# Two SwiGLU feed-forward blocks on one core: a first down part of two groups, and a first Strassen group without down parts

## The chip, the core and the metric

The kernel runs on one core of one Trainium2 chip. The metric is the device time of one execution in microseconds (us), as a median over runs. The engines are named as in the profile: PE (TensorE, matmuls; PEld its weight loads), DVE (VectorE), ACT (ScalarE), POOL (GpSimd) and SP (SyncE, which here only issues DMAs).

## The reference, cut to what matters

One decoder layer on 512 tokens with a model width of 1024. The layer has a feed-forward block (FFN1), a token mixer, a second feed-forward block (FFN2), a gated embedding and a last norm. The change touches only the two feed-forward blocks:

```
def rmsnorm(x, g):
    y = x * rsqrt(mean(x * x) + EPS)
    return y * g

def swiglu(x, w_gate, w_up, w_down):
    return (silu(x @ w_gate) * (x @ w_up)) @ w_down

h = h + 0.5 * swiglu(rmsnorm(h, ffn_norm), w_gate, w_up, w_down)     # D_FF = 2816
```

## The kernel before

**Layout.** Features lie on the 128 partitions and the 512 tokens along the free axis, so h is 8 tiles of 128x512. Float32 products are made of three passes: a weight tile is split into whi (ACT casts it to fp32r, line 416) and wlo (DVE subtracts, line 420), and PE adds whi*xhi, whi*xlo and wlo*xhi. The third of these matmuls is the first that needs wlo. There are three whi and three wlo buffers, and one of each in a second pair, whix and wlox, which most down parts use.

**Groups.** The 2816 hidden features of a feed-forward block are 11 groups of 256. Group 0 is computed plainly, in four products of 24 matmuls with 512 columns (`plain_steps`): gate and up, each with the upper and the lower half of the features. The other groups are computed with a Strassen scheme: seven products P1 to P7 (`Group.steps`), each of 24 matmuls with 256 columns (line 603). Their inputs are sums and differences of halves of x ("forms") and of weight blocks. In FFN1 the forms are made step by step (`Early`, lines 514 to 545), in FFN2 beforehand except one (`t1`, lines 462 to 466). The weight sums are partly made by POOL DMAs that add in place (lines 618, 621 and, after P6's split, 655), and one by DVE (line 613).

**Behind a group's products** come the elementwise steps of `Group`: `seed` (ACT, line 717), `keep_p7` and `keep_u2` (ACT, 721 and 725), for each half a gate sum (DVE, 735), the gate's product with r (DVE, 740), silu (ACT, 741), a product with r (DVE, 745), `finish` with the up part (DVE, 750), and at the end `parts_of_g`, which splits the group's g into ghi (ACT, 760) and glo (DVE, 761). r is the norm's factor per token: `Norm.behind` hangs its three steps on three successive products: sums over the features (PE, line 261), then rsqrt and a diagonal matrix (DVE, 217 to 222 and 280) spread by PE (291), then a copy of r (ACT, 297) with group 0's gate (`plain_gate`, DVE 707, ACT 708). Group 0's g is completed by `plain_finish` (DVE, 713 and 714) and split by `parts_of_g`. A g tile has one buffer, tag "g".

**Down parts.** The down projection is done in six parts over the hidden features. `G_PARTS = (1, 2, 2, 2, 2, 2)` says how many groups each holds. A part is four down steps, each for two of the 8 output tiles: 12 matmuls of 512 columns for each group in the part. A down step loads its weights into rawd (two buffers), splits them, and afterwards DVE adds the result to h (line 795). It is queued some steps after its groups are done: part 0 (group 0 alone) lies among the products of groups 1 and 2, part 1 (groups 1 and 2) among those of groups 3 and 4, and so on. Within a group the order is 1, 7, down, 6, 4, 5, down, 2, 3; for group 1 it is 1, 7, 2, 6, 4, down, 5, down, 3.

**The order of work** is written out by hand. `run` walks through the list of steps. While product i is put into PE's queue, the weights of step i+6 are put into SP's queue, the split of step i+2 and the DVE sum of step i+3 into those of ACT and DVE, and the "after" work of step i-1 likewise: ahead of the split if step i-1 is marked urgent (P1, P7, P6, P3 and the lower plain products), behind it otherwise. A second after-function, where there is one, comes two products later, ahead of both. PE, ACT, DVE and SP each execute in that order; POOL's DMAs are placed by the scheduler.

**Banks.** PSUM has three "mm" banks for the x and q sums of the groups (and one plain up product), two single banks a0 and a1, and three "sm" banks for down steps and norms. A new mm tile takes the bank that was given back first: in this program the q tiles of the groups 1 to 10 lie in one bank throughout and the x tiles in the two others by turns.

## Time and profile before

| | us |
|---|---|
| median of 3 runs | 1108.12 |
| lowest, highest | 1106.18, 1108.39 |
| the profiled execution, its own time | 1107.29 |
| its span, first to last instruction | 1105.6 |
| DVE busy | 783.3 |
| ACT busy | 520.6 |

The profiled execution spends 1.7 us outside its span. The profile's lines give the line number in the kernel, the engine, the operation and the tiles ("out<-in"), so "DVE L420 wlo<-rawb,whi" is the split of a weight tile that lay in rawb. In a timeline, the first column is the start in us from the span's start, the second the length, and the bracket at the end tells how long the engine was idle before the instruction and what released it. Instructions on one engine may overlap slightly, so that the distance from start to start is what an instruction costs its queue. FFN1's plain products begin at 18 us, its Strassen groups at 45; FFN2's Strassen groups begin at 733.

### The profile page before, as it was taken

The numbers are of one execution on the slowest core, as the hardware profiler recorded it, in microseconds if no ns is written. First come the engines' busy times: TensorE is split into PE (matmuls) and PEld (weight loads), VectorE is DVE, ScalarE is ACT, GpSimd is POOL, SyncE is SP. The second block draws the span as 40 slices with busy tenths as digits, with TensorE's granted clock in tenths as the row PEclk, the third lists the DMA queues.
The fourth block names the chain that finished last, engine by engine and source line by source line (L and its number), as shares of the span: only waits on it lengthen the run. The fifth ranks groups of instructions, "written<-read, shape, count | busy, mean of one in ns | idle before, by whom it ended". The sixth has DMA issues, their size and how long they took to land.

```text
span 1105.6 us, 16432 instructions
## 1 busy us (share of the span) xinstructions
PE 1083.8 (98%) x6639; PEld 956.4 (87%) x6639; DVE 783.3 (71%) x1066; ACT 520.6 (47%) x715; POOL 136.9 (12%) x130
## 2 busy tenths in 40 slices
PE   9989999999999999999979999999999999999997
PEld 7879999999998788787858888889999999999887
DVE  6887776766666686766878665768767766667766
ACT  5645444444444455474564343454443443434554
POOL 2001000000000300143213100000000000000311
PEclk9999999999999999999989999999999999999999
DMA  9667757566623322444422323477667667543412
GB/s 365 191 170 205 194 152 191 159 190 155 168 58 114 95 95 80 133 134 134 134 76 77 95 77 114 141 183 202 184 186 191 181 177 185 154 133 108 140 51 77
DMA packets 49036, 161.66 MB, mean 146 GB/s; under 512 B 5568, under 2 KB 5824, under 8 KB 48960
## 3 DMA queue, kind: packets, MB, share of 16 engines
q1 hardware_dynamic: 34128, 117.46, 31.0%
q0 software_dynamic: 9232, 33.56, 16.9%
q10 hardware_dynamic: 5600, 9.60, 2.9%
q8 instruction: 52, 0.85, 0.3%
q14 instruction: 24, 0.20, 0.1%
HBM read 156.33 MB, written 4.26 MB: 145 GB/s over the span
## 4 chain that ended last, share of the span: by engine, by line
PE 85%; DVE 8%; ACT 4%; issue 2%; DMA 0%; SPq 0%; DVEq 0%; ACTq 0%
PE mm L603 18%; PE a L603 14%; PE sm L200 10%; PE sm L201 10%; PE sm L199 10%; PE mm L200 4%; PE mm L199 4%; PE mm L201 4%; PE a L199 3%; PE a L201 3%; PE a L200 3%; DVE wlo L420 1%; ACT whi L416 1%; PE sm L261 1%; DVE tmp L1591 1%
## 5 line engine op out<-in xcount | busy, mean ns | idle before, releaser
L416 ACT CAST whi<-raw 128x1024 fp32r<-128x1024 f32 x138 | 144.3, 1046 | 171.1 <-issue 60.2
L420 DVE TENSOR_TENSOR wlo<-raw,whi 128x1024 fp32r<-128x1024 f32 x137 | 172.9, 1262 | 67.8 <-ACT whi L416 63.9
L603 PE MATMUL mm<-xfb,whi 128*128 128x256 f32 x960 | 166.3, 276 | 0.0
L603 PEld LDWEIGHTS mm<-xfb,whi 128*128 128x128 f32 x960 | 145.9, 188 | 1.6
L603 PE MATMUL mm<-xfb,wlo 128*128 128x256 f32 x480 | 132.8, 277 | 0.0
L201 PE MATMUL sm<-ghi,wlox 128*128 128x512 f32 x296 | 116.3, 393 | 0.0
L200 PE MATMUL sm<-glo,whix 128*128 128x512 f32 x296 | 115.9, 391 | 0.0
L199 PE MATMUL sm<-ghi,whix 128*128 128x512 f32 x296 | 115.1, 389 | 0.0
L603 PE MATMUL a<-xfb,whi 128*128 128x256 f32 x640 | 111.1, 276 | 0.0
L603 PEld LDWEIGHTS a<-xfb,whi 128*128 128x128 f32 x640 | 97.7, 188 | 1.9 <-issue 0.2
L603 PEld LDWEIGHTS mm<-xfb,wlo 128*128 128x128 f32 x480 | 90.1, 188 | 0.0
L603 PE MATMUL a<-xfb,wlo 128*128 128x256 f32 x320 | 88.6, 277 | 0.3 <-DVE wlo L420 0.3
L420 DVE TENSOR_TENSOR wlox<-rawd,whix 128x1024 fp32r<-128x1024 f32 (+1 forms) x40 | 45.7, 1141 | 57.6 <-ACT whix L416 57.6
L420 DVE TENSOR_TENSOR wlo<-rawb,whi 128x1024 fp32r<-128x1024 f32 x52 | 63.6, 1223 | 20.8 <-ACT whi L416 20.8
L741 ACT ACTIVATE g<-g 128x512 f32<-128x512 f32 x40 | 25.3, 632 | 110.8 <-DVE g L740 110.8
L795 DVE SCALAR_TENSOR_TENSOR h<-sm,h 128x512 f32<-128x512 f32 x96 | 63.3, 684 | 6.4 <-PE sm L201 5.7
L416 ACT CAST whi<-rawb 128x1024 fp32r<-128x1024 f32 x52 | 54.2, 1043 | 26.4 <-DVE rawb L613 19.7
L618 POOL DMA_DIRECT2D raw<-in_ffn_gu x20 | 17.4, 869 | 395.5 <-DMA raw<-in_ffn_gu 100.0
L201 PEld LDWEIGHTS sm<-ghi,wlox 128*128 128x128 f32 x296 | 55.5, 188 | 11.7
L200 PEld LDWEIGHTS sm<-glo,whix 128*128 128x128 f32 x296 | 55.5, 188 | 10.9
L199 PEld LDWEIGHTS sm<-ghi,whix 128*128 128x128 f32 x296 | 55.6, 188 | 10.7
L603 PEld LDWEIGHTS a<-xfb,wlo 128*128 128x128 f32 x320 | 60.1, 188 | 0.7 <-DVE wlo L420 0.5
(413 smaller groups left out, 2527.9 us busy)
## 6 DMA issues: line engine op xcount, KB each, us to landing
raw<-in_ffn_gu SPq DMA_DIRECT2D x56, 512.0 KB, 6.0
rawd<-in_ffn_down SPq DMA_DIRECT2D x40, 512.0 KB, 4.0
rawb<-in_ffn_gu SPq DMA_DIRECT2D x32, 512.0 KB, 5.3
raw<-in_ffn_gu POOLq DMA_DIRECT2D x30, 512.0 KB, 5.5
raw<-in_w_in SPq DMA_DIRECT2D x29, 512.0 KB, 3.6
s<-in_ffn_gu SPq DMA_DIRECT2D x20, 512.0 KB, 7.2
s<-in_ffn_gu POOLq DMA_DIRECT2D x20, 512.0 KB, 8.5
raw<-in_w_out SPq DMA_DIRECT2D x16, 512.0 KB, 3.6
```

The costliest lines, as they stand in the source:

```text
L199: nc.tensor.matmul(ps, whi, xhi, start=first, stop=False)
L200: nc.tensor.matmul(ps, whi, xlo, start=False, stop=False)
L201: nc.tensor.matmul(ps, wlo, xhi, start=False, stop=last)
L261: nc.tensor.matmul(ps[:, c : c + 1], part[:, c * P : (c + 1) * P], ones[:, 0:1], start=part is t, stop=part is not t or more is None,)
L416: nc.scalar.copy(self.hi[:, : self.n], self.raw[:, : self.n])
L420: nc.vector.tensor_tensor(self.lo[:, :n], self.raw[:, :n], self.hi[:, :n].bitcast(F32), ALU.subtract)
L603: nc.tensor.matmul(o, wt[:, c], xt, start=fresh and p == m == n == 0, stop=last and n == 2, skip_group_check=True,)
L618: nc.gpsimd.dma_start(w21.raw, self.src[0], accum_op=ALU.add)
L741: nc.scalar.activation(t, t, AF.Silu)
L795: nc.vector.scalar_tensor_tensor(h[d], ps[d], 0.5, h[d], ALU.mult, ALU.add)
L1591: engine.tensor_tensor(t, t, emb[d][:, tok], ALU.mult)
```

## The change

The first two parts change places: part 0 now holds groups 0 and 1, part 1 group 2 alone. The order of the steps is written out as strings: group 1 runs 1, 7, 2, 6, 4, 5 without a down step; then comes P1 of group 2, then P3 of group 1; then group 2's 7, 6, down, 4, 5, down, 2, 3, down; then group 3's 1, down, 7, down, 6, 4, 5, down, 2, 3; from group 4 on the order is as before. The numbers of matmuls, splits and additions to h are the same.

In FFN1 (`at` is now 2 instead of 1) the three steps of the norm are hung one product later: the sums come after the last plain product instead of before it. Group 0's g lies in the tile "embt" instead of "g" (embt held embedding results that POOL stores to DRAM early). `plain_finish` is queued with the split of P5 instead of P4, and group 0's `parts_of_g` behind P3 of group 1, after that group's own `finish` and split, instead of behind P2. In FFN2 (`at` is 0 before and after) these stay where they were. The host's layout of the down weights follows G_PARTS.

```
-G_PARTS = (1, 2, 2, 2, 2, 2)
+G_PARTS = (2, 1, 2, 2, 2, 2)
...
         def plain_gate(self):
-            self.g = sb("g", (P, 2, 2, HT))
+            self.g = sb(self.shared["g0"], (P, 2, 2, HT))
...
-        shared = {}
+
+        shared = {"g0": "embt" if at else "g"}
...
         steps = groups[0].plain_steps()
-        g0, pending = 0, []
+
+
+        g0, downs = 0, []
         for part, n in enumerate(G_PARTS):
-            if part:
-                for j in range(g0, g0 + n):
-
-                    here = pending[: -(-len(pending) // (g0 + n - j))]
-                    pending = pending[len(here) :]
-                    for i in (1, 7, 2, 6, 4, 5, 3) if j == 1 else (1, 7, 6, 4, 5, 2, 3):
-                        steps.append(gs[j][i])
-                        if i in ((5, 4) if j == 1 else (7, 5)):
-                            steps.append(here.pop(0))
             g0 += n
             last = part == len(G_PARTS) - 1
-            each = 2
             mine = groups[g0 - n : g0]
-            pending = [down(part, mine, i, each, last) for i in range(ND // each)]
-        steps += pending
+            downs += [down(part, mine, i, 2, last) for i in range(ND // 2)]
+        order = [(1, "172645"), (2, "1"), (1, "3"), (2, "76d45d23d"), (3, "1d7d645d23")]
+        order += [(j, "17d645d23") for j in range(4, len(groups))]
+        for j, products in order:
+            for i in products:
+                steps.append(downs.pop(0) if i == "d" else gs[j][int(i)])
+        steps += downs
...
         if at:
-            also(steps[8], "split", groups[0].plain_finish)
+            also(steps[9], "split", groups[0].plain_finish)
         else:
             also(steps[3], "after", groups[0].plain_finish)
-        also(steps[6 if at else 4], "after", lambda: groups[0].parts_of_g(slice(0, 2)))
+        also(steps[11 if at else 4], "after", lambda: groups[0].parts_of_g(slice(0, 2)))
...
     steps, mix_norm = swiglu(
         "ffn1", x_ffn1, ffn1_norm, lambda: open_region("left", "mix_left"),
-        splitter("mix_norm", x_mix), 1,
+        splitter("mix_norm", x_mix), 2,
     )
```

## The prediction

> **What bounds the kernel now.** I read the page first, then the waits of PE between 30 and 70 us, then busy time by stretch, then the timelines of DVE and ACT there.

> ```profile
> span 1105.6 us, 16432 instructions
> ## 1 busy us (share of the span) xinstructions
> PE 1083.8 (98%) x6639; PEld 956.4 (87%) x6639; DVE 783.3 (71%) x1066; ACT 520.6 (47%) x715; POOL 136.9 (12%) x130
> ```

> PE is the bound: what it does not lose, no other engine can give back. The question is where PE waits near the edited steps. These are all of PE's waits from 30 to 70 us:

> ```profile
> PE sm L199 <- ACT ghi L760: 2.7, 1, 2.7
> PE sm L261 <- DVE ssum L251: 1.3, 1, 1.3
> PE sm L200 <- DVE glo L761: 0.8, 1, 0.8
> ```

> L261 is the norm's sums, L199 and L200 the first down part, which waits for group 0's g in two parts. Next come stretches (columns: length, PE, PEld, DVE, ACT and POOL busy, granted clock, DMA):

> ```profile
> 33.76:37.17 3.41, 2.09 (x14) 1.52 (x12) 3.10 (x5) 1.57 (x2) 0.00 (x0) 1.00 1.02 365
> 37.17:40.58 3.41, 3.41 (x10) 2.73 (x11) 3.22 (x9) 2.52 (x4) 0.37 (x1) 0.50 0.54 221
> 57.65:61.07 3.42, 1.98 (x17) 1.77 (x16) 3.30 (x6) 1.48 (x3) 0.00 (x0) 1.00 0.40 78
> 61.07:64.48 3.41, 1.39 (x5) 0.94 (x6) 3.04 (x4) 3.16 (x5) 0.00 (x0) 1.00 0.22 72
> 64.48:67.89 3.41, 3.41 (x10) 2.63 (x9) 2.62 (x5) 0.90 (x2) 0.00 (x0) 0.50 0.41 73
> 34.85:100.95 66.10, 61.32 (x420) 56.13 (x419) 54.67 (x78) 31.51 (x43) 5.68 (x7) 0.95 0.64 177
> 41.68:44.48 2.80, 2.80 (x14) 2.26 (x13) 2.15 (x4) 0.04 (x1) 0.68 (x1) 1.00 0.90 164
> 92.74:95.51 2.77, 2.77 (x15) 2.25 (x13) 2.38 (x3) 1.05 (x2) 0.00 (x0) 1.00 0.40 161
> 95.51:98.23 2.72, 2.72 (x26) 2.72 (x24) 1.74 (x4) 1.57 (x2) 0.00 (x0) 1.00 0.74 244
> 733.09:783.02 49.93, 49.59 (x385) 47.16 (x384) 42.57 (x56) 25.08 (x34) 3.84 (x5) 1.00 0.72 195
> ```

> The last five are: FFN1 from the last plain half-product to the end of group 2; half of that plain product (2.80); a small down part (2.77); a Strassen product (2.72); FFN2's groups 1 and 2. PE is idle 4.8 us in FFN1's stretch and only 0.3 in FFN2's. Each of two waits of FFN1 is followed by 3.41 us at clock 0.50, which costs half of it, 1.7, again. So FFN1 has about 8 us to win and FFN2 nothing. In the stretch 61.07:64.48 DVE is busy for 3.04 of 3.41 while PE is idle: DVE is the one that is late.

> **The change, as moves.** Matmuls, casts and additions stay the same in number and nearly in size, so the sum is one of order. (1) In FFN1 the norm's sums come after the last plain product. (2) Group 1 loses its two small down parts; ten Strassen products (seven of group 1, then P1, P7, P6 of group 2) run with no down part between. (3) The first down part is now 24 matmuls and needs group 1's g. In FFN1 it also needs group 0's, which is split right behind it.

> Move 1 removes 1.3 of wait and a 1.7 slow stretch on PE. But r then comes later, and what takes time after it is DVE's queue. Move 2 takes 4 x 2.77 of work from PE at a place where DVE is the slower engine: a Strassen product gives DVE 2.72 us, while its weight split, its share of the group's elementwise steps and the forms cost as much or more. So I follow DVE's order, in both FFNs, until the first down part has its weights.

> ```profile
> 36.32 1.12 PE L261 MATMUL sm<-ones,ssum 128*128 128x1 f32 x8 [1.32 <-DVE ssum L251]
> ```

> ```profile
> 39.90 0.16 DVE L217 TENSOR_SCALAR nv<-sm 128x4 f32<-128x4 f32 x1
> ...
> 42.75 1.22 DVE L420 TENSOR_TENSOR wlo<-raw,whi 128x1024 fp32r<-128x1024 f32 x1
> 46.15 1.29 DVE L707 TENSOR_TENSOR g<-sm,rall 128x512 f32<-128x512 f32 x2 [2.19 <-ACT rall L297]
> ...
> 56.23 0.69 DVE L713 TENSOR_TENSOR g<-g,rall 128x512 f32<-128x512 f32 x1
> ...
> 58.88 0.68 DVE L543 TENSOR_TENSOR ghi<-ghi 128x512 f32<-128x512 f32 x1
> ...
> 61.45 0.68 DVE L420 TENSOR_TENSOR wlo<-rawd,whi 128x512 fp32r<-128x512 f32 x1
> ...
> 65.48 0.68 DVE L735 TENSOR_TENSOR g<-mm,u 128x512 f32<-128x512 f32 x1
> 66.20 0.69 DVE L740 SCALAR_TENSOR_TENSOR g<-g,rall 128x512 f32<-128x512 f32 x1
> 67.65 0.69 DVE L745 TENSOR_TENSOR g<-g,rall 128x512 f32<-128x512 f32 x1 [0.76 <-ACT g L741]
> 68.59 1.23 DVE L420 TENSOR_TENSOR wlo<-rawb,whi 128x1024 fp32r<-128x1024 f32 x1 [0.24 <-ACT whi L416]
> 69.73 1.28 DVE L795 SCALAR_TENSOR_TENSOR h<-sm,h 128x512 f32<-128x512 f32 x2
> ...
> 744.67 0.68 DVE L420 TENSOR_TENSOR wlo<-rawd,whi 128x512 fp32r<-128x512 f32 x1
> ...
> 761.33 1.23 DVE L761 TENSOR_TENSOR glo<-g,ghi 128x1024 fp32r<-128x1024 f32 x1 [1.12 <-ACT ghi L760]
> ```

> ```profile
> 45.53 0.59 ACT L297 COPY rall<-sm 128x512 f32<-128x512 f32 x1 [3.81 <-PE sm L291]
> 46.88 1.23 ACT L708 ACTIVATE g<-g 128x512 f32<-128x512 f32 x2 [0.76 <-DVE g L707]
> 48.01 1.03 ACT L416 CAST whi<-rawb 128x1024 fp32r<-128x1024 f32 x1
> ```

> From one start to the next: a wide step (L420, L761, the L613 sum) 1.14 (68.59 to 69.73); a narrow one 0.6; rsqrt with diagonals 2.85 (39.90 to 42.75); group 0's finish 2.65 (56.23 to 58.88); one pair of forms with its splits 2.57 (58.88 to 61.45), of which forming and splitting 1.2 each; gate sum to gate 0.72, gate to the product with r 1.45 since silu lies between, then 0.94 to the next split (67.65 to 68.59); finish of a g to its L761 1.8 (0.68 and a wait of 1.12). ACT's cast is 1.03.

> **FFN1.** Until 39.90 DVE runs as before. Then, each time being the end of the step named:
> P7's split comes first now, at 41.4 (39.90, an estimated 0.3 for the end of its cast, 1.14). PE takes the last plain product from 34.85 to 40.45 (2 x 2.80), and the sums to 41.5 (about 1.1, as the row has it). So rsqrt and diagonals run from 41.5 to 44.35, and PE's spread follows P1 (to 44.2) with a wait of 0.2. DVE goes on with P4's form 45.5, P2's split 46.65 and P6's sum L613 47.8; r has been copied by then (46.1), so the two gate products with r follow at once: 49.0. Now P6's split needs its cast, which on ACT stands behind both silus: the first starts 0.73 after the products with r begin, the cast 1.13 later (46.15, 46.88, 48.01), ends 1.03 after that, at 50.7. DVE stands 1.7 us, and P6's split is done at 51.85, where PE wanted it at 50.6. The splits of P4's form 53.05, P4 54.3, P5's pair of forms 56.9, P5 58.4 (a wait of 0.35 for its cast, behind the copies of the forms), group 0's finish 61.05, group 2's P1 62.2, P3 63.3. Gate sum and gate 64.6, the product with r, behind silu, starts at 65.45, and 0.94 later P7 of group 2: 67.55. L613 68.7; the second gate sum, gate and finish 70.6. The cast for P6 of group 2 now has a silu (0.63, an estimate as half of the row's 1.23), the seed of group 2 and its own 1.03 to come on ACT, so that split is done at 73.4. Finish of group 1 and, 1.8 after its start, L761: 76.35. Group 0's L761 77.5, the down part's split 78.7. PE's third matmul of the down part needs it: 78.75. Left are 22/24 of 5.54 (twice 2.77), P4, P5, a second down part, P2 and P3: 78.75 + 5.08 + 4 x 2.72 + 5.54 = 100.25. Before, the same work was done at 100.95: **-0.7**.

> **FFN2.** At 744.67 DVE is done with the forms, and takes P5's split instead of a down part's: 746.0. Group 2's P1 747.5. P3's cast waits for the whi buffer of P4's product (PE from 733.09, five products, 746.7), so its split ends at 749.15. Then as above: gates, P7 of group 2 753.3, L613 754.45, gates and finish 756.4, product with r, P6 of group 2 759.15 (PE wanted it at 757.8), finish and L761 762.1, the down part's split 763.3. PE wanted it at 733.09 + 27.2 + 0.46 = 760.75. Same remainder: 763.35 + 21.5 = 784.85 against 783.02: **+1.8**.

> Costed at nothing: SP's first rawd load, now behind group 2's weights, whose last buffer is free after P7's split at 41.4, has 35 us of cover; POOL's addition for P3 (L655) is issued behind P6's split at 51.85 and has 7 us until P3's cast, past which ACT, and so every silu, would be late by as much; group 0's g in the embt tile follows a store issued before the sums; group 2's P7 takes the mm bank that the gate sum freed at 64, and if it were x's, freed at 70.6, P7 would start 3 us later and the down part still wait for DVE till 78.7. After it DVE has a 24-matmul product to catch up in, and PE sets the pace again; d2 and d3, one product apart, share one whix buffer, whose cast and split (2.3) fit in P1's 2.72.

> Sum: -0.7 + 1.8 = +1.1. The profiled execution took 1107.29, so 1108.4; the median of the runs shown, 1108.12, is 0.8 above it, so 1109.2.

> **Clock.** The rows: idle time of 2.02 (61.07:64.48) was followed by a slow stretch, of 1.44 (57.65:61.07) by none, and of 1.32 with single-column sums for the rest (33.76:37.17) by one. [...] I go by the rows.

> **Rivals.** *Faster: DVE does not wait for ACT.* Of the walk's 38.8 us, 32.7 are DVE's own steps (14 wide ones at 1.14, 2.85, 4.97 of forms, 1.2, 2.65 and 5 of gates) and 6.1 are waits for silu, casts and PE; in FFN2 4.3 are. If half go, FFN1 comes to -3.8 and FFN2 to -0.2: 1104.1. If all go, -6.8 and, since PE is the bound then (760.75 in place of 763.35), -0.8: 1100.5. For it: 8 us of waits are there to win. Against: on ACT each cast stands behind the silu of the same step, in order.

> *Slower: the clock.* PE waits 3 us for group 2's P6 and 2.3 for the first down part in FFN1. If one 3.41 us window holds about 2 us of idle time (1.44 does not do) and the slow one falls on the down part, behind which DVE sets nothing, it costs 1.7: 1110.9; in FFN2, where the waits are 1.3 and 1.2, another 1.7: 1112.6. Against: a slow window between the two waits is hidden.

> *No effect of its own:* FFN1 gains as much as FFN2 loses: within 1 us of 1108.1. It belongs to the forecast's case.

> **Numbers.** Forecast 0.49, its own range 1107.5 to 1110.5; faster rival 0.28; slower rival 0.23. About 0.2% (2.2 us) is what a measurement can tell here. All of the faster case and none of the forecast's is below that; of the slower one nearly all is above, and a little of the forecast. So faster 0.28, same 0.46, slower 0.26. The range leaves out the better half of the faster case and two slow windows: 1104.0 to 1111.5.

> **What would show it.** Right: no wait at L261; in FFN1 the first down part's third matmul near 78.7 with L201 waiting for DVE wlo; PE waits in P6 of groups 1 and 2; new waits of 1 to 2.6 us in FFN2 near 758 and 762; the end of group 2's P3 near 100.2 and, less FFN1's gain, 784.1. Wrong: the first down part in FFN1 before 75 (faster case), or clock 0.50 in the stretch that holds it (slower case).

## The result, and the profile after

| | before | after |
|---|---|---|
| median of 5 runs, us | 1107.73 | 1116.47 |
| lowest, highest | 1106.18, 1108.39 | 1114.0, 1118.22 |
| profiled execution | 1107.29 | 1114.13 |
| its span | 1105.6 | 1112.4 |

The change is slower: the ratio is 1.0077 (95% interval 1.0061 to 1.0092), or 8.5 us, where +1.1 was forecast. (Two later executions, one of e5 and one of e10, took 1206 and 2199 us; they lie far from all others and are left out, and so is the profile of e5, taken on one of them.)

The head of the page after, first:

```profile
span 1112.4 us, 16429 instructions
...
PE 1083.2 (97%) x6639; PEld 955.7 (86%) x6639; DVE 783.6 (70%) x1066; ACT 521.1 (47%) x715; POOL 136.9 (12%) x130
```

No engine has much more to do than before: DVE's busy time rose by 0.3 us and ACT's by 0.5, and PE's fell by 0.6. The 6.8 us of span come from the order. Next, the largest waits of PE between 36 and 125 us, FFN1's groups 1 to 3 (columns: total us, times, longest):

```profile
PE a L603 <- DVE g L735: 4.3, 1, 4.3
PE sm L199 <- DVE h L796: 1.2, 1, 1.2
PE a L603 <- DVE wlo L420: 1.0, 2, 0.7
PE mm L603 <- DVE wlo L420: 0.7, 1, 0.7
```

and all of them between 730 and 830 us, in FFN2:

```profile
PE a L603 <- DVE g L735: 2.9, 1, 2.9
PE sm L199 <- DVE h L796: 1.2, 1, 1.2
```

The old waits of FFN1 (L261, 1.3; L199, 2.7; L200, 0.8) are gone. Two new ones, L735 and L796, stand in both feed-forward blocks, and neither is for weights or for g: both are for a *bank* that DVE has still to read. Here are the stretches that locate the loss (columns as in the prediction):

```profile
34.83:101.51 66.68, 60.09 (x420) 55.24 (x418) 53.46 (x74) 31.64 (x41) 5.15 (x6) 0.97 0.55 146
...
69.64:73.05 3.41, 3.40 (x16) 3.41 (x17) 2.55 (x4) 2.09 (x3) 0.00 (x0) 0.50 0.02 5
...
117.95:122.15 4.20, 3.04 (x14) 2.17 (x13) 3.37 (x4) 3.17 (x4) 2.60 (x3) 1.00 0.97 238
...
735.26:787.95 52.69, 49.78 (x385) 47.52 (x384) 41.55 (x51) 25.05 (x32) 3.47 (x4) 1.00 0.55 146
...
804.39:808.61 4.22, 3.06 (x15) 2.18 (x14) 3.39 (x4) 3.17 (x4) 2.62 (x3) 1.00 0.95 228
```

FFN1 up to the end of group 2 takes 66.68 against 66.10 (+0.6). The first small down part of FFN1's group 3 takes 4.20 where a small part without a wait takes 2.77 (+1.4). FFN2's groups 1 and 2 take 52.69 against 49.93 (+2.8). The small part of FFN2's group 3 takes 4.22 (+1.4). That is 6.2 of 6.8. Of the rest, 0.3 is in FFN2's group 4, where three products between 833.22 and 841.71 take 2.83 us each in place of 2.72; the other 0.3 is spread in small pieces. From the end of that group on the two traces run side by side, 6.8 apart.

**The wait of 4.3.** DVE's timeline in FFN1, after:

```profile
50.90 1.23 DVE L420 TENSOR_TENSOR wlo<-rawb,whi 128x1024 fp32r<-128x1024 f32 x1 [1.64 <-ACT whi L416]
...
65.61 0.69 DVE L745 TENSOR_TENSOR g<-g,rall 128x512 f32<-128x512 f32 x1 [0.70 <-ACT g L741]
66.54 1.23 DVE L420 TENSOR_TENSOR wlo<-raw,whi 128x1024 fp32r<-128x1024 f32 x1 [0.24 <-ACT whi L416]
67.68 1.22 DVE L613 TENSOR_TENSOR raw<-raw,s 128x1024 f32<-128x1024 f32 x1
68.82 0.68 DVE L735 TENSOR_TENSOR g<-a,p 128x512 f32<-128x512 f32 x1
...
74.27 0.69 DVE L750 TENSOR_TENSOR g<-g,a 128x512 f32<-128x512 f32 x1 [0.66 <-PE a L603]
...
78.36 1.22 DVE L420 TENSOR_TENSOR wlo<-rawd,whi 128x1024 fp32r<-128x1024 f32 x1
```

and PE's, at its two waits for L735:

```profile
69.65 0.55 PE L603 MATMUL a<-xfb,whi 128*128 128x256 f32 x1 [4.29 <-DVE g L735]
...
757.38 0.47 PE L603 MATMUL a<-xfb,whi 128*128 128x256 f32 x2 [2.91 <-DVE g L735]
```

The second gate sum of group 1 (68.82) reads bank a; P3 of group 1 adds its own product to the same bank. On DVE the gate sum is queued behind the split for P7 of group 2 and the L613 sum, and only then may P3 start. Before, a small down part lay between P5 and P3; these two rows are the gate sum and the start of P3 in the trace of before:

```profile
72.06 0.68 DVE L735 TENSOR_TENSOR g<-a,p 128x512 f32<-128x512 f32 x1
```

```profile
73.40 0.39 PE L603 MATMUL a<-xfb,whi 128*128 128x256 f32 x2
```

P3 started 1.3 us after the gate sum began, and nothing waited.

**The wait of 1.2.** DVE in FFN1's group 3, after, and the matmul of PE that it holds up, the first for the second output tile of that down step:

```profile
116.44 1.22 DVE L613 TENSOR_TENSOR rawb<-rawb,s 128x1024 f32<-128x1024 f32 x1
118.78 1.23 DVE L420 TENSOR_TENSOR wlo<-rawb,whi 128x1024 fp32r<-128x1024 f32 x1 [1.11 <-ACT whi L416]
119.92 1.28 DVE L796 SCALAR_TENSOR_TENSOR h<-sm,h 128x512 f32<-128x512 f32 x2
```

```profile
120.66 0.50 PE L199 MATMUL sm<-ghi,whix 128*128 128x512 f32 x1 [1.16 <-DVE h L796]
```

There are three sm banks and a down step takes two. "d7d" in the order of group 3 puts two down steps one product apart; the second needs a bank that the first one's addition to h (L796) has yet to read. That addition stands behind P6's split, which stands 1.11 us for its cast.

### The profile page after: what moved, and what is told of

Its sections match the earlier page's. It is cut to its first block, busy times and chain, and to the rows that moved or that the text cites. A ratio compares the mean times of both kernels' runs of the same rounds, so it can differ in the third digit from the quotient of the medians.

```text
span 1112.4 us, 16429 instructions
## 1 busy us (share of the span) xinstructions
PE 1083.2 (97%) x6639; PEld 955.7 (86%) x6639; DVE 783.6 (70%) x1066; ACT 521.1 (47%) x715; POOL 136.9 (12%) x130
## 4 chain that ended last, share of the span: by engine, by line
PE 84%; DVE 9%; ACT 4%; issue 2%; DMA 1%; SPq 0%; DVEq 0%; ACTq 0%
PE mm L603 18%; PE a L603 14%; PE sm L199 10%; PE sm L200 10%; PE sm L201 10%; PE mm L200 4%; PE mm L199 4%; PE mm L201 4%; PE a L199 2%; PE a L201 2%; PE a L200 2%; DVE wlo L420 2%; ACT whi L416 1%; DVE tmp L1589 1%; DVE ya L1412 1%
## 5 line engine op out<-in xcount | busy, mean ns | idle before, releaser
L416 ACT CAST whi<-raw 128x1024 fp32r<-128x1024 f32 x138 | 144.3, 1046 | 158.1 <-issue 50.2
L420 DVE TENSOR_TENSOR wlo<-raw,whi 128x1024 fp32r<-128x1024 f32 x137 | 172.9, 1262 | 62.5 <-ACT whi L416 58.9
L199 PE MATMUL sm<-ghi,whix 128*128 128x512 f32 x288 | 112.2, 390 | 2.3 <-DVE h L796 2.3
L201 PE MATMUL sm<-ghi,wlox 128*128 128x512 f32 x288 | 113.2, 393 | 0.0
L200 PE MATMUL sm<-glo,whix 128*128 128x512 f32 x288 | 112.8, 392 | 0.0
L420 DVE TENSOR_TENSOR wlox<-rawd,whix 128x1024 fp32r<-128x1024 f32 (+1 forms) x40 | 44.6, 1116 | 65.7 <-ACT whix L416 65.7
L741 ACT ACTIVATE g<-g 128x512 f32<-128x512 f32 x40 | 25.3, 632 | 113.4 <-DVE g L740 113.4
L420 DVE TENSOR_TENSOR wlo<-rawb,whi 128x1024 fp32r<-128x1024 f32 x52 | 63.6, 1223 | 20.9 <-ACT whi L416 20.8
L416 ACT CAST whi<-rawb 128x1024 fp32r<-128x1024 f32 x52 | 54.3, 1043 | 30.1 <-DVE rawb L613 17.5
L796 DVE SCALAR_TENSOR_TENSOR h<-sm,h 128x512 f32<-128x512 f32 x96 | 63.0, 684 | 7.2 <-PE sm L201 6.8
L199 PEld LDWEIGHTS sm<-ghi,whix 128*128 128x128 f32 x288 | 54.1, 188 | 13.5 <-DVE h L796 3.2
L201 PEld LDWEIGHTS sm<-ghi,wlox 128*128 128x128 f32 x288 | 54.1, 188 | 11.4
L200 PEld LDWEIGHTS sm<-glo,whix 128*128 128x128 f32 x288 | 54.0, 188 | 10.5
```

Source lines behind the costliest of these rows:

```text
L199: nc.tensor.matmul(ps, whi, xhi, start=first, stop=False)
L200: nc.tensor.matmul(ps, whi, xlo, start=False, stop=False)
L201: nc.tensor.matmul(ps, wlo, xhi, start=False, stop=last)
L416: nc.scalar.copy(self.hi[:, : self.n], self.raw[:, : self.n])
L420: nc.vector.tensor_tensor(self.lo[:, :n], self.raw[:, :n], self.hi[:, :n].bitcast(F32), ALU.subtract)
L741: nc.scalar.activation(t, t, AF.Silu)
```

## The experiments

Theory **"DVE is late"** (the prediction's): DVE and its hand-offs with ACT set when the first down part gets its weights, so the wait before P3 costs little by itself; mended, PE waits elsewhere. Rival **"bank alone"**: without the bank's wait the 4.3 and 2.9 us come back. A third, **"clock"**: the waits cost by the slow windows behind them.

### e1: the two small down steps further apart

```diff
-        order = [..., (2, "76d45d23d"), (3, "1d7d645d23")]
+        order = [..., (2, "76d45d23d"), (3, "1d76d45d23")]
```

> The changed kernel with only group 3's order altered: 1, down, 7, 6, down, 4, 5, down, 2, 3 in place of 1, down, 7, down, 6, 4, 5, down, 2, 3. In the changed kernel's profile PE stands 1.16 us in each FFN before the second of these down parts, released by the addition to h of the one before (sm banks: three, two for each down part). If that wait is a loss of its own, both waits go and the span falls by 2.4 to 2.9 us (the small part took 4.20 and 4.21 in place of 2.77). If it only takes up slack that a later step would need anyway, the wait reappears elsewhere in group 3 and the span stays within 0.7 us.

1113.02 us, ratio 1.0056 (1.0043 to 1.0069); both waits for L796 are gone, and the two blocks take 2.77 each in the trace of e1. That is 0.0021, 2.3 us, less than the change, with intervals that overlap a little. The waits of 1.2 and the blocks of 4.20 and 4.22 are shown to be the sm bank's.

### e2: the gate sum ahead of the split

P5 of group 1 is made urgent, so its "after" work, the gate sum, goes ahead of the split queued in that step.

```diff
-            s = Step(..., i in (1, 7, 6, 3))
+            s = Step(..., i in (1, 7, 6, 3) or (self.j == 1 and i == 5))
```

> The changed kernel, but group 1's second gate sum, gate and finish are queued ahead of the split of group 2's P7 and of the L613 sum instead of behind them. Theory bank: P3 adds to the bank that this gate sum still has to read, and the 4.29 us (FFN1) and 2.91 us (FFN2) that PE stands before P3 are the loss; with the gate sum earlier by a wide split and a wide sum (2.3) plus what lies around, P3 starts 2.6 us earlier in each FFN and the end of group 2 comes 2.5 to 2.9 us earlier in each, over 5 us in all. Theory DVE late: the queue of DVE up to the first down part's split is the same length in either order, so the wait goes back into P7, P6 and the down part: P3 starts 2.6 earlier, the first down part's third matmul only 0.5 to 1.0 earlier in each FFN, 1 to 2 us in all, plus up to 1.7 for each slow clock window that no longer falls there.

1115.1 us, 1.0066 (1.0054 to 1.0079). DVE's gate sum, PE's wait at the third matmul of the first down part, and FFN2's stretch, in the trace of e2:

```profile
66.00 0.68 DVE L735 TENSOR_TENSOR g<-a,p 128x512 f32<-128x512 f32 x1
```

```profile
79.06 0.50 PE L201 MATMUL sm<-ghi,wlo 128*128 128x512 f32 x1 [0.64 <-DVE wlo L420]
```

```profile
735.52:787.77 52.25, 50.59 (x386) 47.56 (x385) 41.46 (x51) 25.00 (x32) 3.46 (x4) 1.00 0.56 147
```

and PE's waits there, between 730 and 830 us:

```profile
PE sm L199 <- DVE h L796: 1.2, 1, 1.2
PE sm L201 <- DVE wlo L420: 0.7, 1, 0.7
PE a L603 <- DVE wlo L420: 0.4, 1, 0.4
PE a L603 <- DVE g L735: 0.3, 1, 0.3
PE mm L603 <- DVE wlo L420: 0.2, 1, 0.2
```

The gate sum is 2.8 us earlier, and P3 starts at 66.83 in place of 69.65, after a wait for bank a that is still 1.8 long. Yet the third matmul of the down part comes at 79.06 instead of 79.98, and FFN2's groups 1 and 2 take 52.25 instead of 52.69. In FFN2 the wait for bank a fell from 2.9 to 0.3, and PE waits for weights instead: in P7 and P6 of group 2 and at L201, where "DVE is late" has them. Bank alone falls: of the 2.8 us by which P3 starts earlier 0.9 come back in FFN1, though a slow window went with them (mean clock 1.00 from 34.83 to 100.69 in e2, where the changed kernel has 0.97 to 101.51), and in FFN2 0.4 of 2.6. The mend has a price of its own, though. The cast for P7's split now stands behind a silu on ACT, DVE waits 1.04 for it in place of 0.25, and in FFN2 the down part's split ends 30.58 us after group 1's first product starts, in place of 30.19. So 0.4 is what this edit brings, not all that the bank cost.

### e3: the change in FFN1 only

FFN2 keeps the parts and the order of before.

```diff
+PARTS = {"ffn1": (2, 1, 2, 2, 2, 2), "ffn2": (1, 2, 2, 2, 2, 2)}
...
-        for part, n in enumerate(G_PARTS):
+        for part, n in enumerate(PARTS[name]):
...
+        if PARTS[name][0] == 1:
+            order = [(1, "17264d5d3")] + [(j, "17d645d23") for j in range(2, len(groups))]
```

> The change in FFN1 alone; FFN2 has the parts and the order of before. By the traces FFN2's stretch from P1 of group 1 to P1 of group 5 lost 4.2 us (2.8 up to the end of group 2, 1.4 at the small down parts), FFN1's 2.0, of 6.8 in all. So 4 to 4.5 us faster than the changed kernel and about 2 to 3 slower than before. If FFN2's loss were given back later in the trace, or FFN1's clock windows carried most of the time, it would stay within 2 us of the changed kernel.

1110.74 us, 1.0032 (1.002 to 1.0043), +3.5 us. Its waits are FFN1's of the change (4.4 and 1.2). The 3.5 is more than the 2 to 3 expected: in its trace 6.83 us of slow clock follow the first wait, where the change's trace has 3.41. So a good part of the loss is FFN2's.

### e4: only the norm one product later

The kernel before with one edit.

```diff
-        splitter("mix_norm", x_mix), 1,
+        splitter("mix_norm", x_mix), 2,
```

> Before, with one part of the change: FFN1's norm sums one product later (at = 2); parts, order, tiles and the places of group 0's finish and split as before. If PE's waits are what counts, 1.3 us of wait and 1.7 of slow clock at the sums go: 3 us faster. Theory DVE late: r comes 1.8 later, DVE's queue follows it, and of the 3 us about half is lost again before the first down part: its second matmul, at 63.6 before, at about 62, so 1.5 to 2 us faster. If the later r cost the first down part as much as the sums gain, no difference.

1105.87 us, 0.9993 (0.9984 to 1.0002). FFN1 to the end of group 2, and what is left of the waits between 36 and 125 us:

```profile
34.83:99.58 64.75, 60.47 (x419) 55.20 (x418) 54.77 (x79) 31.72 (x43) 5.73 (x7) 0.95 0.65 181
```

```profile
PE sm L199 <- ACT ghi L760: 2.9, 1, 2.9
PE a L603 <- DVE wlo L420: 0.5, 1, 0.5
PE sm L200 <- DVE glo L761: 0.5, 1, 0.5
```

In the profiled executions this is 1.35 us shorter than before; the timing can't tell it from no change. Move 1 by itself is the half of the change that does not hurt.

### e5: both mends together

The edits of e1 and e2 on the changed kernel.

> The changed kernel with both waits mended: group 3's down parts one product further apart and group 1's second gate sum ahead of the splits. Theory two waits and DVE late: the two mends add (2.9 for the parts, 1.7 for the gate sums, by the traces of the runs that did one each), so 4 to 5 us faster than the changed kernel, but still 2 to 4 slower than before, since DVE's queue sets the first down part in both FFNs. If the two waits were the whole loss, it would come out at before's time or below it, by the 3 us of the norm's sums.

1.0038 (1.0024 to 1.0051), five runs from 1109.93 to 1112.07. The two mends bring back about 4.3 us of the change's 8.5, from the two banks and the slow clock behind the first, less what the mend of e2 costs; 4.2 stay.

### e6: is DVE too full, or waiting?

e2, with group 1's low half of g (its L761) left out and ghi used in its place: a part of the computation is missing, so that 1.14 us of DVE are gone right ahead of the down part's split.

```diff
-            nc.vector.tensor_tensor(lo, g, hi.bitcast(F32), ALU.subtract)
+            if self.j != 1:
+                nc.vector.tensor_tensor(lo, g, hi.bitcast(F32), ALU.subtract)
```

> The changed kernel with group 1's second gate sum ahead of the splits, and group 1's DVE step L761 (glo) left out: its down part multiplies by ghi a second time, so the low part of group 1 is missing from the output; PE's work is the same. Theory DVE late: that step lies in DVE's queue right ahead of the first down part's weight split, so the first down part's third matmul comes 1.1 us earlier in each FFN than in the run with the step (79.06 and 766.1 there, the latter shifted by FFN1's gain too), until PE itself is the bound. If the bank alone was the loss, it stays where it was.

1113.02 us, 1.0053 (1.0038 to 1.0068). DVE's next step and ACT's casts, in the trace of e6 (where the L761 of before is L762):

```profile
76.44 1.23 DVE L762 TENSOR_TENSOR glo<-embt,ghi 128x1024 fp32r<-128x1024 f32 x1 [2.06 <-ACT ghi L760]
```

```profile
74.41 1.05 ACT L760 CAST ghi<-g 128x1024 fp32r<-128x1024 f32 x1 [1.89 <-DVE g L750]
75.36 1.04 ACT L760 CAST ghi<-embt 128x1024 fp32r<-128x1024 f32 x1
76.31 1.04 ACT L416 CAST whi<-rawd 128x1024 fp32r<-128x1024 f32 x1
```

The third matmul moved from 79.06 to 78.86, not by 1.1: DVE's wait before that step grew from 1.11 to 2.06. At this place DVE is not full. What sets the time is a chain to and fro: DVE's split for P6 of group 2 (which stands 0.57 for its cast), group 1's finish behind it (L750, at 73.69, without a wait for PE), three casts on ACT in order, DVE's split for the down part.

### e7: FFN1 changed with both mends, FFN2 as before

The edits of e3 and e1, and that of e2 in FFN1 alone.

> FFN1 as in the changed kernel with both mends, FFN2 as before. FFN1 lost 2.0 by the traces; the mends give 1.4 for the parts, 0.9 for the gate sums and a slow clock window or two that falls away: 0.3 to 2 us faster than before, 1105 to 1106.5. If DVE is as late as ever and the clock windows come back elsewhere, the same as before.

1107.68 us, 1.0008 (0.9999 to 1.0017). The stretch to the end of group 2:

```profile
34.88:100.94 66.06, 60.00 (x420) 54.03 (x419) 53.22 (x74) 31.55 (x41) 5.15 (x6) 1.00 0.55 146
```

66.06 against 66.10 before. There is no slow window left in it (1.00), and PE's idle time in it rose from 4.8 to 6.1 us. My 0.3 to 2 us faster failed: even mended, the change has nothing for FFN1. The profiled execution, 1108.79, has a span 1.5 longer than before, but only 0.4 of that is FFN1's. Another 1.0 is lost in the mixer, between the two blocks, where a slow window falls on full work; the same stretch in the trace of e7 and in that of before:

```profile
576.12:579.53 3.41, 3.41 (x9) 2.63 (x8) 1.34 (x3) 3.38 (x9) 0.00 (x0) 0.50 0.43 154
```

```profile
576.12:579.53 3.41, 3.41 (x16) 2.83 (x16) 1.07 (x2) 3.38 (x8) 0.00 (x0) 1.00 0.50 154
```

The trace of e2 has this window too (1.1 lost), that of the change does not.

### e8: the first down part behind P5 of group 1

The parts of before, with the norm late, g0 in embt, group 0's split moved forward and group 1's gate sums ahead of the splits; the first part lies behind more products of group 1. Of the edit, the order and the places of group 0's steps:

```diff
-                        if i in ((5, 4) if j == 1 else (7, 5)):
+                        if i in (((5, 3) if at else (5, 4)) if j == 1 else (7, 5)):
...
-            also(steps[8], "split", groups[0].plain_finish)
+            also(steps[9], "split", groups[0].plain_finish)
+            also(steps[10], "split", lambda: groups[0].parts_of_g(slice(0, 2)))
```

> Before's parts (one group first) with, in FFN1 alone: the norm's sums one product later, group 0's g in the embt tile, its finish queued with P5's split and its own split with the first down part's, the order of group 1 as 1, 7, 2, 6, 4, 5, down, 3, down, and group 1's gate sums ahead of the splits. Theory DVE late: what PE has to wait for DVE falls only by what is moved behind P5: in the run with the sums late alone PE stood 2.9 and 0.5 before the first down part and ran two slow windows; here about 2 before the first down part and 1 to 1.5 before P3, so group 2's P1 begins 1 to 2 us earlier than there: 1104 to 1105.5. If the norm's and the first down part's waits were all, 6 us faster than before.

1108.25 us, 1.0011 (1.0003 to 1.0019): a miss. Between 36 and 90 us seven waits of 0.3 to 1.1 us, from bank a (1.1) to an sm bank (0.4), take the place of the old ones.

### e9: e4, with a form later

The form that P4's split makes (copies and splits of `Early.form(1)`) is partly moved out of the way of group 0's finish, and group 1's gate sum forward as in e2.

```diff
-    for k, i in ((4, 3), (6, 2), (10, 1)):
+    for k, i in ((4, 3), (6, 2)):
...
+    also(steps[10], "split", lambda: Early.form(early, 1))
+    ahead(steps[12], "split", lambda: Early.t(early, 1, True))
```

> Before, with FFN1's norm sums one product later, as in the run with that part alone, and two more steps of FFN1 moved: the copies and splits of P5's pair of forms behind group 0's split (only the forming stays ahead of it), and group 1's second gate sum ahead of the splits. Theory DVE and ACT late: group 0's low part, which the first down part waits for, comes 1.2 us earlier, P5 has its inputs while that down part runs, so of 2.9 + 0.5 of waiting about 1.5 goes, and one of the two slow clock windows: 1 to 3 us faster than that run, 1103 to 1105 on the scale where before is 1106.7. If the chain through ACT is what sets the first down part, and P3 then waits for the gate sum, it stays within 0.7 of it.

1106.11 us, 0.9991 (0.9982 to 0.9999). The wait for ghi fell from 2.9 to 1.3, and the others, 0.5 and 0.5 in e4, rose to 2.6 together; between 36 and 125 us:

```profile
PE a L603 <- DVE wlo L420: 1.5, 2, 0.7
PE sm L199 <- ACT ghi L760: 1.3, 1, 1.3
PE sm L200 <- DVE glo L761: 0.8, 1, 0.8
PE sm L201 <- DVE wlox L420: 0.3, 1, 0.3
```

It is as good as e4, not better, where 1 to 3 us were expected. Of all kernels run these two are the lowest, about 1 us below before, at the edge of what can be told.

### e10 and e12: the change in FFN2 only

As e3 with the two lists exchanged, and FFN1's norm and group 0 as before. e12 is the same kernel once more.

> The change in FFN2 alone (parts and order; nothing else of it touches FFN2); FFN1 as before. Theory so far: FFN2 loses 2.8 us before the end of group 2 (P3 behind the gate sum) and 1.4 at group 3's small down parts, and sometimes a slow clock window more after P3's wait of 2.9: 4 to 6 us slower than before. If the two FFNs' losses were not independent (FFN1's shift of the clock windows making FFN2's), it would be within 2 us of before.

> The change in FFN2 alone, unaltered, for one more profile: its executions lay at 1110.6 and 1111.5 (clock 0.992 to 0.993) and at 1115.3 to 1117.2 (0.986 to 0.988). Theory clock window: in the slower heap FFN2's wait before P3 is followed by one slow window and the rest of the surplus lies in further slow windows elsewhere, the waits being the same. Rival: longer waits in FFN2.

Five runs of e10: 1110.57, 1111.51, 1115.3, 1115.85, 1117.2 (before 1107.37; ratio 1.0071, 1.0055 to 1.0088); e12: 1110.4. The times fall into two heaps. The lower one is 3.2 to 4.1 above before; its waits in FFN2 are those of the change, 2.91 and 1.16, and no slow window follows the 2.91. With e3's 3.5 that makes 6.7 to 7.6, where the profiled execution of the change lost 6.8: so far the blocks add up. With the median of all five runs, 7.9 above before, they would make 11.4, more than the change's 8.5; so that they add up is shown for the lower heap alone, and the 4 to 6 expected lie for the most part between the heaps. The runs of the upper heap have a mean clock of 0.986 to 0.988 against 0.992 and 0.993. Both traces that were taken fell in the lower heap, so where the upper heap loses its 5 us stays open.

### e11: the changed kernel once more

> The changed kernel unaltered, for one more profile: its five executions lay in two heaps, 1114 at a mean clock of 0.993 and 1116.5 to 1118.2 at 0.989 to 0.990, and only one of the first kind has a trace. If it is one of the slower heap: theory clock window, the surplus is slow windows of 3.41 us behind P3's two waits (4.3 and 2.9), one or two each, 1.7 us for each, and the waits themselves are as in the first trace. Rival: the waits themselves are longer there (a later DMA or DVE queue).

1115.48 us with the same waits (4.36, 2.91, 1.16). Granted clock behind the first wait, and ahead of and behind the start of P3 in FFN2, in the trace of e11:

```profile
68.06:74.89 6.83, 5.53 (x26) 5.57 (x27) 4.39 (x7) 2.08 (x3) 0.86 (x1) 0.50 0.01 2
```

```profile
754.14:757.55 3.41, 0.99 (x9) 0.79 (x7) 3.16 (x4) 0.76 (x1) 0.00 (x0) 1.00 0.00 0
757.55:760.96 3.41, 2.92 (x14) 2.95 (x15) 2.51 (x5) 2.08 (x3) 0.00 (x0) 0.50 0.02 5
```

and in the first trace of the change the window ahead of FFN1's slow one, two windows that share FFN2's wait, and the 3.41 us behind that wait:

```profile
66.23:69.64 3.41, 0.00 (x0) 0.02 (x1) 3.13 (x5) 0.28 (x1) 0.00 (x0) 1.00 0.00 0
752.31:755.72 3.41, 2.16 (x20) 1.96 (x18) 2.46 (x4) 1.57 (x2) 0.00 (x0) 1.00 0.00 0
755.72:759.13 3.41, 1.75 (x15) 1.77 (x16) 3.27 (x5) 1.13 (x3) 0.00 (x0) 1.00 0.02 5
757.38:760.79 3.41, 3.40 (x29) 3.41 (x30) 2.54 (x4) 2.09 (x3) 0.00 (x0) 1.00 0.02 5
```

The first trace had one slow window behind FFN1's wait and none behind FFN2's; this one has two and one, and is 1.35 us longer. The same wait costs clock in one execution and none in the other, and the rows show what differs. In the first trace the slow stretches begin at 69.64 and 561.16, 491.52 us or 144 windows apart; counted on in such steps, an edge falls at 755.72, in the middle of FFN2's wait, and PE stands 1.25 in one window and 1.66 in the next. In e11 one window holds 2.42 of the wait, and the next is slow. That supports slow windows as the source of the spread from 1114.0 to 1118.2 (clocks from 0.993 down to 0.989), though the slowest executions were not traced.

## Why the prediction was wrong

**DVE's walk was right.** The steps, each by its end (the start of the next), predicted and then measured:

| step | predicted | after |
|---|---|---|
| FFN1: split for P6 of group 1 | 51.85 | 52.04 |
| first product with r, start | 65.45 | 65.61 |
| split for P7 of group 2 | 67.55 | 67.68 |
| L613 | 68.7 | 68.82 |
| split for the down part | 78.7 | 79.5 |
| FFN2 (plus its later start, 2.17): L613 | 756.62 | 756.56 |
| the down part's split | 765.47 | 765.45 |

Up to the gate sum nothing is off by more than 0.3 us, waits for casts included. L261's wait went, and P6 of group 1 waited (0.7).

**The step that failed** is the list under "Costed at nothing". It weighed "group 2's P7 takes the mm bank that the gate sum freed" and stopped at the mm banks. P3 of group 1 needs bank a, and the walk itself had the gate sum that frees it after 68.7. With that, P3 starts at 69.65 and P7 and P6 behind it, and the slow clock in P3's window, 3.41 us at 0.50, adds half of it, 1.7: 69.65 + 3 x 2.72 + 1.7 = 79.51, which is where the down part begins. The third matmul ran at 79.98 against 78.75, and the end of group 2 is off by the same: 101.51 against 100.25. Without the slow clock PE would have come at 77.8, ahead of the weights; it took both. P3, so late and so slow, even holds up DVE, whose finish of group 1 stood 0.66 us for it (74.27), and DVE's split for the down part came 0.8 late. An estimate from these rows: with P3 at full speed DVE would not have stood, the split would have come 0.66 earlier, and the third matmul at about 79.0. So of the 1.2 about 0.2 is the wait by itself and 1.0 the slow window behind it, and the two belong together: in all four traces with this wait of 4.3 to 4.4 (after, e1, e3, e11) one or two slow windows follow it (3.41 us after, 6.83 in each of the others), and in e2 and e7, where it is 1.8, the granted clock is 1.00 throughout that stretch. In FFN2 DVE kept its times to 0.1 us and PE itself came late, by the wait before P3: 766.41 for the third matmul against 765.52 forecast (with the 2.17), 787.95 at the end against 787.02. These two terms were mis-sized by 1.3 and 0.9: the sum's -0.7 was +0.6, and +1.8 was +2.8.

**"PE sets the pace again" behind the first down part** was wrong by 1.4 in each block. The prediction looked at the closeness of d2 and d3, the third and the fourth step of the first part, and checked the whix buffer. The sm banks run out one step later, between the fourth step and the next part's first, which lie one product apart too and which it did not weigh. Together: 1.3 + 0.9 + 1.4 + 1.4 = 5.0 of the 5.7 by which the profiled execution missed +1.1. e1 shows the last two.

**The faster rival** fell: of the waits on ACT in the walk none went, and e6 shows why. Taking a step from DVE there mostly lengthens its wait for ACT (1.14 taken, 0.2 won). (In that rival's sum, half of FFN2's waits gives -0.3 and not -0.2; nothing rests on it.)

**The slower rival**, the clock, was half right. The windows do occur, but behind the wait before P3, and not behind P6 or the down part, as it had them. The one in FFN1 cost PE 1.7 in the profiled execution, of which by the estimate above about 1.0 counted; in the five timed runs such windows are probably the 2.3 us between that execution and the median, which no trace shows.

**What held** is the thesis that PE cannot win here, since DVE and ACT set the first down part: with the bank mended (e2) the third matmul of the down part still came at 79.06, and with both mends FFN1 stands about where it stood before (e7). What remains of the loss in e5, 4.2 us, is FFN2's lateness for 2.3 (52.25 against 49.93, in e2, the price of that mend included). How the other 1.9 is made up was not measured, since e5 has no usable trace; e7's trace has 0.4 in FFN1 and 1.0 in the mixer's slow window, which would be most of it.

## What to carry to other kernels

When work between two products is moved away, list for every bank that the later product writes its last reader, and where that reader stands in its engine's queue; buffers of weights are only half of the list. A down step that takes two of three banks must not follow another before the addition that empties them has had its turn (PE stood 1.16 us for it here). And price a mended wait by what is late next: here P3 of group 1 came 2.8 us earlier and 0.9 came back.

## What the runs showed of the hardware

How long PE stands within one window goes with what follows it. From 10 us after the start on, there are six windows at full clock in the two traces in which PE stood 2.02 us or more, and each was followed by a slow one: 2.02, 2.80 and 3.41 before (from 61.07, 556.00 and 1098.72), and 3.41, 2.42 and 2.30 after (from 66.23, 557.75 and 1103.88). In e11 the window of 2.42 from 754.14 was, too. In all other windows at full clock of the two traces PE stood 1.66 or less, and only one of them was followed by a slow one: that of 1.32 with single-column sums, in the kernel before, which the prediction shows. Those of 1.44 (from 57.65, before) and of 1.57 and 1.66 (from 574.81 and 755.72, after) were not. (PE's busy time is taken as the profile models it.) So a wait of 4.3, however it falls, leaves at least 2.1 in one window or fills one, and a wait of 2.91 was followed by a slow window where 2.42 of it lay in one (e11) and by none where it was split into 1.25 and 1.66 (the first trace).

Two executions of one program then differ though their waits are nearly the same (4.3, 2.9 and 1.2 in the first trace of the changed kernel, 4.4, 2.9 and 1.2 in e11): these two are 1.35 us apart, and the first has one slow window in the feed-forward blocks (from 69.64), e11 three (two from 68.06, one from 757.55). For the whole spread, 1114.0 to 1118.2 with clocks of 0.993 and 0.989, the same cause is likely but not shown. The kernel before, with waits of its own in FFN1, spread over 2.2 us.
